# Layer 1's expert input weights read four rows to a partition, norm columns in that order, in a two-layer trunk kernel

## The chip, the cores and the metric

One core of a Trainium2 chip. The time is device microseconds of one execution. Before the change it was 2333.3 us (median of three runs, 2330.22 to 2333.62).

## The reference

A trunk of two layers on 1024 tokens of 1024 features, all in float32. Layer 0 has a pooling mixer, layer 1 chunked gated linear attention, and each is followed by a mixture of 64 experts. Cut to what matters here:

```python
for i in range(DEPTH):
    mod = (silu(c) @ w_mod[i] + b_mod[i])[:, None, :]
    shift1, scale1, gate1, shift2, scale2, gate2 = jnp.split(mod, 6, axis=-1)
    h = rmsnorm(x, norm_gain[i, 0]) * (1.0 + scale1) + shift1
    x = x + gate1 * (pool_mixer(h, ...) if i % 2 == 0 else gla_mixer(h, ...))
    h = rmsnorm(x, norm_gain[i, 1]) * (1.0 + scale2) + shift2
    x = x + gate2 * hier_moe(h, w_group, b_group, w_expert, b_expert, w_in, w_out)
return rmsnorm(x, final_norm_g)

def hier_moe(h, ...):          # top-1 of 8 groups, top-2 of its 8 experts for each token
    ...
    xs = t[token_of]           # tokens sorted by expert
    gu = lax.ragged_dot(xs, w_in, group_sizes)        # w_in: 1024 x 768 an expert
    gate, up = jnp.split(gu, 2, axis=-1)
    ys = lax.ragged_dot(silu(gate) * up, w_out, group_sizes)   # w_out: 384 x 1024
    ys = ys * weights.reshape(-1)[order][:, None]
    return jnp.zeros_like(t).at[token_of].add(ys)
```

The product with w_in sums over the 1024 features, so the features may be taken in any order if tokens and weights have the same one.

## The kernel before

The kernel works layer by layer: mixer, router, experts. A norm makes tokens without scale and shift, which go to a table h_d in DRAM; the per-feature scale (1 + scale2) times gain and the shift are kept as columns, feature on the partition, eight columns of 128 (`modA[:, l, 1, :]` and `sec(l, 3)`), and are applied behind the transposes in front of an expert. The sums are kept in DRAM, in x_d, to which each expert adds.

An expert is handled in a pass over at most 64 of its tokens; experts with more (the kernel looks at the counts that the router left) have a second pass. In layer 1, 64 experts make 68 passes. In one pass:

- POOL's `gather` (line 470) reads the tokens' rows from h_d into one of eight buffers XG: partitions 0 to 63 hold the features 0 to 511, partitions 64 to 127 the features 512 to 1023.
- `expert_in` has four transposes of 128x128 on PE (line 480), each of 128 consecutive columns of XG, and applies scale and shift to the results, on ACT for odd (line 488) and on DVE for even ones (line 490).
- `expert_first` has 32 matmuls with w_in (line 506), gate and up on the two halves of the partitions. ACT makes the SiLU (line 513), DVE the product with up (line 514).
- `expert_turn` transposes the hidden values on PE (line 522; its three read every third column, a step of 12 B) and ACT copies them (line 523). `expert_last` has 12 matmuls with w_out (line 531).
- DVE scales the result by the router's weight (line 536), and POOL adds the rows to x_d with a scatter (line 537).

On PE the order is written out: the next expert's transposes stand between its matmuls of `expert_first` and those of `expert_turn`, while ACT and DVE make the hidden values. On the other engines a scheduler orders the instructions at build time. On POOL, one scatter waits until the scatter before it has landed, since both add to x_d, and the gather for eight experts later stands between two scatters, since it writes the buffer that the scatter has read out. Gathers for second passes, where there is one, are made under a branch, `na` experts ahead (4).

The weights come on SP's queue, three loads of 1.573 MB an expert into a ring of 14 slots of 128 x 3072 floats: w_in in two halves (line 466) and w_out (line 467). A partition of a w_in slot gets four rows of w_in that lie 128 rows apart, in four runs of 3,072 B; a partition of w_out gets three consecutive rows, one run of 12,288 B. `queued` holds each load until the load three before it has landed, so that gathers and scatters find room on the DMA engines, which both share with the loads. Loads for layer 1's first experts are made while the mixer still runs (`fill1`).

In layer 1's mixer a loop over t handles eight tiles of 128 tokens, with the router one or two tiles behind; PE is in written order here too. Tokens of the tiles go through DRAM, and POOL fetches them with gathers (qk_d on line 1105, v_d on line 1109, r_d on line 1113, x_d on line 1114).

Of the kernel before, what the change touches and what calls it, by code (L numbers as in the profile page):

```python
# [36 lines left out]
def trunk_kernel(ctx, tc, x_in, c_in, norm_gain, w_mod, b_mod, pool_w, pool_b, pool_scale,  # L37
# [15 lines left out]
    v_d = dram.tile([SEQ, 1024], F32, name="v_d")  # L53
    r_d = dram.tile([SEQ, 1024], F32, name="r_d")
    z_d = dram.tile([SEQ, 16], F32, name="z_d")

    def part(slot, kb, n):
        a = int(kb * 256)
# [2 lines left out]
    def ps():  # L61
        return psum.tile([128, 512], F32, name="ps")
# [101 lines left out]
    def mod_scale(l, s):  # L164
        V.scalar_tensor_tensor(modA[:, l, s, :], mod[:, l, 24 * s + 8:24 * s + 16], 1.0,
                               C1[:, 96 + (2 * l + s) * 8:96 + (2 * l + s) * 8 + 8], op0=OP.add, op1=OP.mult)

    def sec(l, s):
        return mod[:, l, 8 * s:8 * s + 8]

    def row(col, half, diag):
        d = diag.rearrange("p (a b) -> p a b", a=4)
# [273 lines left out]
    hv = h_d.rearrange("t (g d) -> (t g) d", g=2)  # L446
    yv = [y.rearrange("t (g d) -> (t g) d", g=2) for y in x_d]

    def expert_load(win, wout, sl):
        behind.clear()  # L450
        for j in range(3):
            third_load(win, wout, j, sl)

    behind = []

    def queued(ins):

        if len(behind) >= DEEP:
            tc.add_manual_dep(ins.ins, behind[-DEEP].name, DATA_SYNC, reason="loads leave room for gathers")
        behind.append(ins.ins)  # L460
        return ins

    def third_load(win, wout, j, sl):
        if j < 2:
            src = win.rearrange("(k p) f -> p k f", p=128)
            return [queued(SP.dma_start(A[sl[j]].rearrange("p (k f) -> p k f", k=4), src[:, 4 * j:4 * j + 4]))]
        return [queued(SP.dma_start(A[sl[2]], wout.rearrange("(p c) d -> p (c d)", c=3)))]
# [8 lines left out]
    def expert_in(l, i, g, first=None):  # L476
        xT = part(15, 2 * i, 512).rearrange("p (c g t) -> p c g t", c=4, g=2)
        pp = [ps(), ps()]
        for cc in range(4):
            T.transpose(pp[cc % 2][:, cc // 2 * 128:cc // 2 * 128 + 128], XG[g][:, cc * 128:(cc + 1) * 128], ident)  # L480
        with tc.issue_after(first()) if first else ExitStack():
            for cc in range(4):
                pv = pp[cc % 2][:, cc // 2 * 128:cc // 2 * 128 + 128].rearrange("p (g t) -> p g t", g=2)
                for g in range(2):
                    kc = 4 * g + cc
                    sc, sh = modA[:, l, 1, kc:kc + 1], sec(l, 3)[:, kc:kc + 1]
                    if cc % 2:
                        S.activation(xT[:, cc, g, :], pv[:, g, :], AF.Identity, bias=sh, scale=sc)  # L488
                    else:
                        ins = V.tensor_scalar(xT[:, cc, g, :], pv[:, g, :], sc, sh, op0=OP.mult, op1=OP.add).ins  # L490
        return ins
# [146 lines left out]
    def rest(l, lo, hi, flag, src, sl, bufs):  # L638

        bi, bg = bufs  # L640
        base, en = ov[:, 0:1], ov[:, 1:2]
        pb, R, w = ov[:, 2:10], ov[:, 10:34], ov[:, 34:35]
        Rv = R.rearrange("p (t w) -> p t w", w=3)
        Sl = A[sl[0]][:, 0:512]
        nmax = nc.values_load(flag, min_val=0, max_val=SEQ, skip_runtime_bounds_check_because=COUNT_REASON)
        with tc.If(nmax > 128):
            V.memset(en, float(lo))
            with tc.For_i(lo, hi, 1) as e:
                n = nc.values_load(cnt_i[0:1, bass.ds(e, 1)], min_val=0, max_val=SEQ,
                                   skip_runtime_bounds_check_because=COUNT_REASON)  # L650
                with tc.If(n > 128):
                    V.memset(base, 128.0)
                    with tc.For_i(128, n, 64):
                        p = ps()
                        m = 0
                        for k in range(2):
                            V.tensor_scalar(pb, pos(k), base, None, op0=OP.subtract)
                            slots_of(Sl, pb, 0)
                            V.tensor_scalar(pb, eid(k), en, None, op0=OP.is_equal)
                            for c, a in enumerate((tokno, place, wk(k))):  # L660
                                V.tensor_tensor(Rv[:, :, c], pb, a, op=OP.mult)
                            for t in range(NT):
                                for g in range(2):
                                    T.matmul(p[64 * g:64 * g + 64, 0:3], Sl[:, t * 64:(t + 1) * 64], Rv[:, t, :],
                                             start=m == 0, stop=m == 15)
                                m += 1
                        V.tensor_scalar(ovi, p[:, 0:2], 2.0, gcol, op0=OP.mult, op1=OP.add)
                        V.tensor_copy(w, p[:, 2:3])
                        gather(ovi[:, 0:1], bg)
                        expert_in(l, bi, bg)  # L670
                        expert_load(*src(e), sl)
                        expert_out(l, bi, sl, (w, ovi[:, 1:2]), bg)
                        V.tensor_scalar(base, base, 64.0, None, op0=OP.add)
                V.tensor_scalar(en, en, 1.0, None, op0=OP.add)
# [128 lines left out]
    def load0(e, j, sl):  # L803
        r = e // 8
        if r not in regs:
            regs[r] = nc.values_load(cnt_i[0:1, NE + 16 + r:NE + 17 + r], engines=(ET.SP,), min_val=0, max_val=56,
                                     skip_runtime_bounds_check_because="eight times the number of a group")
        d = bass.ds(regs[r] + e % 8, 1)
        third_load(moe_w_in[0, d].rearrange("o k f -> (o k) f"), moe_w_out[0, d].rearrange("o k f -> (o k) f"), j, sl)

    for s in range(3):
        load0(0, s, RING0[0:3])
# [452 lines left out]
    pulled = [gl_load2(0), gl_load2(1)]  # L1265

    def load1(e, j, sl):
        return third_load(moe_w_in[1, e], moe_w_out[1, e], j, sl)

    def fill1(lo, hi):  # L1270
        for s in range(lo, hi):
# [20 lines left out]
    with tc.manual_schedule(engines={ET.PE}):  # L1292
        for t in range(NT + 2):
            for i in ((0, 1) if t == 0 else (t,) if 1 < t < NT else ()):
                gl_scores(i)
                if t == 0:
                    gl_mix(i)
            if t == 3:
                columns = [late_mod(14, LATE[4])]
            if t == 4:  # L1300
                columns = [late_mod(15, LATE[5])]
            if 0 < t < NT - 1:
                gl_z(t + 1)
            if t == 1:
                columns = [late_mod(10, LATE[0])]
            if t == 2:
                columns = [late_mod(12, LATE[2]), late_mod(13, LATE[3])]
            if 0 < t <= NT:
                gl_out(t - 1, 0)
            while columns:  # L1310
                columns.pop(0)()
            if t == 2:
                mod_scale(1, 1)
            if t > 1:
                route_turn(t - 2, 1, xnb, hTb)
            if t > NT:
                route_logits(t - 2, hTb, wrv, L, brow)
            if 0 < t < NT - 1:
                gl_gate(t + 1)
            if 1 < t < NT:  # L1320
                route_logits(t - 2, hTb, wrv, L, brow)
            if t == NT - 1:
                consts = route_consts(area1)
                r_a = route(1, 0, NT - 2, area1, consts, **held)
                r_b = route(1, NT - 2, NT, area2, consts, **held)
                next(r_a)
            if 1 < t < NT:
                gl_mix(t)
            if t == 1:
                columns = [late_mod(11, LATE[1])]  # L1330
            if t == NT - 1:
                gate2_rows(1, [part(8, 0, 512), part(8, 2, 512)])
            if 0 < t <= NT:
                gl_out(t - 1, 1)
                while columns:
                    columns.pop(0)()
                if t in (3, 4):
                    fill1(3 * t - 9, 3 * t - 6)
                SP.dma_start(x_d[1][(t - 1) * 128:t * 128, :], X[t - 1])
                xn_tile(t - 1, xnb, xnb, 3)  # L1340
            if t == NT:
                route_logits(t - 2, hTb, wrv, L, brow)
                next(r_a)
            if t < NT:
                gl_turn(t)
            if t + 2 < NT:
                gl_load(t + 2)
                gl_load_v(t + 2)
                gl_load2(t + 2)
# [14 lines left out]
                      reason="what is needed sooner goes first")  # L1364
    G.memset(part(15, 7, 1024), 0.0)
    with tc.manual_schedule(engines={ET.PE}):
        moe(1, RING1, MAIN1, (4, 5, 10, 11), load1, AHEAD1, 4)
    rest(1, 0, NE, cnt_i[0:1, NE + 8:NE + 9],
         lambda e: tuple(w[1, bass.ds(e, 1)].rearrange("o k f -> (o k) f") for w in (moe_w_in, moe_w_out)),
         RING1[0:3], (0, 4))  # L1370
# [43 lines left out]
```

## Time and profile before

| | us |
|---|---|
| median of three runs | 2333.3 |
| profiled execution | 2333.5 |
| its span | 2331.8 |
| PE busy | 1983.0 (85%) |
| weight loads of PE busy | 949.8 (41%) |
| DVE busy | 725.9 (31%) |
| ACT busy | 627.2 (27%) |
| POOL busy | 496.3 (21%) |

The span runs from the first to the last instruction; the time of the execution has 1.7 us more. Layer 1's experts take from about 1508 to 2302 us. Behind them the last scatter lands, the result is read back, normed and written. The mean granted clock of TensorE was 0.968 of full speed. Busy shares are means over stages with different limits, so the rows below are of single stages: a window row has the stretch, its length, the busy us of PE, weight loads, DVE, ACT and POOL with their counts, the granted clock, the busy share of the 16 DMA engines and their GB/s. In a timeline row, the figure in brackets is the time that the engine was idle before, with what ended it.

### The profile page before, as it was taken

Reading aid. Unit: us, or ns where it says so; the run is one execution under the profiler, and the core shown is the slowest. Engines: PE = TensorE matmul, PEld = TensorE weight load, DVE = VectorE, ACT = ScalarE, POOL = GpSimd, SP = SyncE. Lnnn points to the kernel's source line nnn. Section 1 sums busy time; section 2 is a strip of 40 time slices with the busy share of each in tenths; the row PEclk is TensorE's granted clock in tenths of the full one; section 3 lists DMA queues with packets and bytes.
Section 4 is the critical chain, followed back from the end, with each engine's and each line's share of the span. In section 5 each row is a group of like instructions: output and inputs, shape, how many; then the busy total and the mean of one; then the engine's idle time right before and its main releaser. Section 6 shows DMA issues by size and latency. Waiting matters only on the chain. (4 is left out here: it accounts for less than half of the span.)

```text
span 2331.8 us, 31439 instructions
## 1 busy us (share of the span) xinstructions
PE 1983.0 (85%) x11243; PEld 949.8 (41%) x11244; DVE 725.9 (31%) x1797; ACT 627.2 (27%) x1433; POOL 496.3 (21%) x422
## 2 busy tenths in 40 slices
PE   7867888899999999999888999888877777778784
PEld 5544333344444444444335665433323333333331
DVE  4463545312121221212137667422212111112122
ACT  4131323222222221313126665222111111112113
POOL 0303222222222222222115110222222212222210
PEclk9988999899999999999998999899999999999997
DMA  9999989998988899999945942699999999999995
GB/s 333 332 329 360 391 289 343 373 354 312 348 311 305 328 358 335 378 331 363 352 139 179 334 157 100 248 394 388 400 381 396 375 379 390 379 387 381 393 381 206
DMA packets 241991, 770.04 MB, mean 330 GB/s; under 512 B 31591, under 2 KB 63757, under 8 KB 224318
## 3 DMA queue, kind: packets, MB, share of 16 engines
q1 hardware_dynamic: 196498, 684.66, 76.1%
q0 software_dynamic: 43856, 77.67, 12.1%
q10 hardware_dynamic: 1372, 4.28, 0.5%
q8 instruction: 154, 2.52, 0.4%
q14 instruction: 111, 0.91, 0.1%
HBM read 735.44 MB, written 69.80 MB: 345 GB/s over the span
## 5 line engine op out<-in xcount | busy, mean ns | idle before, releaser
L506 PE MATMUL ps<-slot,slot 128*64 128x384 f32 x4416 | 755.4, 492 | 94.7 <-DMA slot<-in_moe_w_in_dram 76.5
L506 PEld LDWEIGHTS ps<-slot,slot 128*64 128x64 f32 x4416 | 337.0, 138 | 515.9 <-issue 248.3
L531 PE MATMUL ps<-slot,slot 128*64 128x512 f32 x1656 | 402.8, 623 | 49.3 <-ACT slot L523 42.8
L513 ACT ACTIVATE slot<-ps 64x384 f32<-64x384 f32 x138 | 66.9, 485 | 1261.6 <-PE ps L506 1235.6
L924 PE MATMUL ps<-slot,slot 128*128 128x512 f16 x1152 | 276.4, 386 | 7.2 <-DVEq L1061 5.7
L490 DVE TENSOR_SCALAR slot<-ps,kept 128x64 f32<-128x64 f32 x552 | 151.2, 334 | 339.7 <-PE ps L480 335.6
L514 DVE TENSOR_TENSOR slot<-slot,ps 64x384 f32<-64x384 f32 x138 | 75.9, 550 | 525.5 <-ACT slot L513 512.5
L537 POOL DMA_INDIRECT x_d<-kept x96 | 159.3, 1659 | 348.7 <-DVEq L632 172.4
L531 PEld LDWEIGHTS ps<-slot,slot 128*64 128x64 f32 x1656 | 110.7, 141 | 247.5 <-issue 184.4
L470 POOL DMA_INDIRECT kept<-h_d,kept x96 | 102.0, 1062 | 503.1 <-DMA x_d<-kept 328.3
L488 ACT ACTIVATE slot<-ps,kept 128x64 f32<-128x64 f32 x552 | 178.4, 403 | 70.0 <-PE ps L480 61.4
L536 DVE SCALAR_TENSOR_TENSOR kept<-ps,kept 128x512 f32<-128x512 f32 x96 | 72.0, 750 | 325.3 <-PE ps L531 322.5
L924 PEld LDWEIGHTS <-slot 128*128 128x128 f16 x1152 | 107.6, 99 | 153.4 <-issue 46.1
L522 PE MATMUL ps<-kept,slot 64*128 64x64 f32 x414 | 75.9, 290 | 91.9 <-DVE slot L514 90.6
L522 PEld LDWEIGHTS ps<-kept,slot 64*128 64x128 f32 x414 | 57.8, 202 | 135.8 <-DVE slot L514 101.0
L537 POOL DMA_INDIRECT x_d<-slot,kept x42 | 66.7, 1587 | 163.0 <-DVE slot L536 105.1
L470 POOL DMA_INDIRECT slot<-h_d,kept x42 | 43.8, 1042 | 243.8 <-DMA x_d<-slot,kept 158.4
L1236 PE MATMUL ps<-slot,slot 128*128 128x512 f16 x384 | 85.7, 379 | 1.2 <-DVE slot L1228 1.0
L536 DVE SCALAR_TENSOR_TENSOR slot<-ps,kept 128x512 f32<-128x512 f32 x42 | 31.5, 751 | 122.2 <-PE ps L531 116.3
L480 PE MATMUL ps<-kept 128*128 128x128 f32 x384 | 63.4, 288 | 1.6 <-DMA kept<-h_d,kept 1.3
L480 PEld LDWEIGHTS ps<-kept 128*128 128x128 f32 x384 | 40.6, 141 | 59.1 <-issue 56.7
L1236 PEld LDWEIGHTS <-slot 128*128 128x128 f16 x384 | 37.1, 98 | 46.6 <-issue 2.1
(329 smaller groups left out, 1693.2 us busy)
## 6 DMA issues: line engine op xcount, KB each, us to landing
slot<-in_moe_w_in_dram SPq DMA_DIRECT2D x256, 1536.0 KB
slot<-in_moe_w_out_dram SPq DMA_DIRECT2D x128, 1536.0 KB
slot<-in_w_mod_dram SPq DMA_DIRECT2D x30, 1536.0 KB
slot<-in_gla_w_in_dram SPq DMA_DIRECT2D x8, 1536.0 KB
h_d<-slot POOLq DMA_DIRECT2D x16, 512.0 KB
slot<-in_x_dram SPq DMA_DIRECT2D x8, 512.0 KB
slot<-x_d POOLq DMA_DIRECT2D x8, 512.0 KB
slot<-in_gla_w_out_dram SPq DMA_DIRECT2D x8, 512.0 KB
```

Source lines behind the costliest of these rows:

```text
L470: return G.indirect_dma_start(out=XG[i], out_offset=None, in_=hv, in_offset=bass.IndirectOffsetOnAxis(ap=idx, axis=0), bounds_check=2 * SE ...
L480: T.transpose(pp[cc % 2][:, cc // 2 * 128:cc // 2 * 128 + 128], XG[g][:, cc * 128:(cc + 1) * 128], ident)
L488: S.activation(xT[:, cc, g, :], pv[:, g, :], AF.Identity, bias=sh, scale=sc)
L490: ins = V.tensor_scalar(xT[:, cc, g, :], pv[:, g, :], sc, sh, op0=OP.mult, op1=OP.add).ins
L506: T.matmul(p1[s, 0:384], xT[:, cc, g, :], W[:, u], start=n == 0, stop=n == 7)
L514: return V.tensor_tensor(hh, hh, p1[up, 0:384], op=OP.mult).ins
L522: T.transpose(p3[:, cc * 64:(cc + 1) * 64], hh[:, :, cc], ident[s, s])
L531: T.matmul(p2[g * 64:g * 64 + 64, :], hT[:, cc * 64:(cc + 1) * 64], o[:, cc, g * 512:(g + 1) * 512], start=cc == 0, stop=cc == 2)
L536: V.scalar_tensor_tensor(XG[y], p2, w, G2, op0=OP.mult, op1=OP.mult)
L537: ins = G.indirect_dma_start(out=yv[l], out_offset=bass.IndirectOffsetOnAxis(ap=sidx, axis=0), in_=XG[y], in_offset=None, bounds_check=2 * ...
L924: T.matmul(p, hP[:, m, kc, :], W[:, n, :], start=kc + i == 0, stop=kc == KC - 1 and i == 2)
L1236: T.matmul(p, oT[:, m, kc, :], woh[kc][:, n, half * 512:(half + 1) * 512], start=kc + i == 0, stop=kc == KC - 1 and i == 2)
```

## The change

In layer 1 alone, partition p of a w_in slot now gets four consecutive rows of w_in (4p to 4p + 3 of a half), one run of 12,288 B in place of four of 3,072 B. The tokens' features must come in the same order: each transpose in front of an expert reads every fourth column of XG (a step of 16 B), and the columns of scale and shift must be in that order too. `mod_turn`, called in the mixer's loop at t = 3, makes them: it transposes both sets of eight columns on PE, copies them on DVE, writes them to a small DRAM table m_d and reads them back in the new order into the columns of layer 0, which are no longer used. `expert_in` reads these columns in both layers. The gathers for second passes are made three experts ahead in layer 1, not four.

```diff
--- before.py
+++ after.py
@@ -53,6 +53,7 @@
     v_d = dram.tile([SEQ, 1024], F32, name="v_d")
     r_d = dram.tile([SEQ, 1024], F32, name="r_d")
     z_d = dram.tile([SEQ, 16], F32, name="z_d")
+    m_d = dram.tile([2, 8, 128], F32, name="m_d")
 
     def part(slot, kb, n):
         a = int(kb * 256)
@@ -167,6 +168,17 @@
 
     def sec(l, s):
         return mod[:, l, 8 * s:8 * s + 8]
+
+    def mod_turn(l, scr):
+
+
+        p = ps()
+        T.transpose(p[0:8, 0:128], modA[:, l, 1, :], ident)
+        T.transpose(p[0:8, 128:256], sec(l, 3), ident)
+        V.tensor_copy(scr[0:8, :], p[0:8, 0:256])
+        G.dma_start(m_d.rearrange("v k p -> k v p"), scr[0:8, :].rearrange("k (v p) -> k v p", v=2))
+        for v, a in enumerate((modA[:, 0, 1, :], sec(0, 3))):
+            G.dma_start(a.rearrange("p (g c) -> p g c", g=2), m_d[v].rearrange("(g b) (a c) -> (b a) g c", g=2, c=4))
 
     def row(col, half, diag):
         d = diag.rearrange("p (a b) -> p a b", a=4)
@@ -446,10 +458,10 @@
     hv = h_d.rearrange("t (g d) -> (t g) d", g=2)
     yv = [y.rearrange("t (g d) -> (t g) d", g=2) for y in x_d]
 
-    def expert_load(win, wout, sl):
+    def expert_load(l, win, wout, sl):
         behind.clear()
         for j in range(3):
-            third_load(win, wout, j, sl)
+            third_load(l, win, wout, j, sl)
 
     behind = []
 
@@ -460,7 +472,10 @@
         behind.append(ins.ins)
         return ins
 
-    def third_load(win, wout, j, sl):
+    def third_load(l, win, wout, j, sl):
+
+        if j < 2 and l:
+            return [queued(SP.dma_start(A[sl[j]], win.rearrange("(g p k) f -> p g (k f)", g=2, k=4)[:, j]))]
         if j < 2:
             src = win.rearrange("(k p) f -> p k f", p=128)
             return [queued(SP.dma_start(A[sl[j]].rearrange("p (k f) -> p k f", k=4), src[:, 4 * j:4 * j + 4]))]
@@ -477,13 +492,14 @@
         xT = part(15, 2 * i, 512).rearrange("p (c g t) -> p c g t", c=4, g=2)
         pp = [ps(), ps()]
         for cc in range(4):
-            T.transpose(pp[cc % 2][:, cc // 2 * 128:cc // 2 * 128 + 128], XG[g][:, cc * 128:(cc + 1) * 128], ident)
+            rows = XG[g].rearrange("p (r c) -> p c r", c=4)[:, cc] if l else XG[g][:, cc * 128:(cc + 1) * 128]
+            T.transpose(pp[cc % 2][:, cc // 2 * 128:cc // 2 * 128 + 128], rows, ident)
         with tc.issue_after(first()) if first else ExitStack():
             for cc in range(4):
                 pv = pp[cc % 2][:, cc // 2 * 128:cc // 2 * 128 + 128].rearrange("p (g t) -> p g t", g=2)
                 for g in range(2):
                     kc = 4 * g + cc
-                    sc, sh = modA[:, l, 1, kc:kc + 1], sec(l, 3)[:, kc:kc + 1]
+                    sc, sh = modA[:, 0, 1, kc:kc + 1], sec(0, 3)[:, kc:kc + 1]
                     if cc % 2:
                         S.activation(xT[:, cc, g, :], pv[:, g, :], AF.Identity, bias=sh, scale=sc)
                     else:
@@ -668,7 +684,7 @@
                         V.tensor_copy(w, p[:, 2:3])
                         gather(ovi[:, 0:1], bg)
                         expert_in(l, bi, bg)
-                        expert_load(*src(e), sl)
+                        expert_load(l, *src(e), sl)
                         expert_out(l, bi, sl, (w, ovi[:, 1:2]), bg)
                         V.tensor_scalar(base, base, 64.0, None, op0=OP.add)
                 V.tensor_scalar(en, en, 1.0, None, op0=OP.add)
@@ -806,7 +822,7 @@
             regs[r] = nc.values_load(cnt_i[0:1, NE + 16 + r:NE + 17 + r], engines=(ET.SP,), min_val=0, max_val=56,
                                      skip_runtime_bounds_check_because="eight times the number of a group")
         d = bass.ds(regs[r] + e % 8, 1)
-        third_load(moe_w_in[0, d].rearrange("o k f -> (o k) f"), moe_w_out[0, d].rearrange("o k f -> (o k) f"), j, sl)
+        third_load(0, moe_w_in[0, d].rearrange("o k f -> (o k) f"), moe_w_out[0, d].rearrange("o k f -> (o k) f"), j, sl)
 
     for s in range(3):
         load0(0, s, RING0[0:3])
@@ -1265,7 +1281,7 @@
     pulled = [gl_load2(0), gl_load2(1)]
 
     def load1(e, j, sl):
-        return third_load(moe_w_in[1, e], moe_w_out[1, e], j, sl)
+        return third_load(1, moe_w_in[1, e], moe_w_out[1, e], j, sl)
 
     def fill1(lo, hi):
         for s in range(lo, hi):
@@ -1311,6 +1327,8 @@
                 columns.pop(0)()
             if t == 2:
                 mod_scale(1, 1)
+            if t == 3:
+                mod_turn(1, part(4, 11, 256))
             if t > 1:
                 route_turn(t - 2, 1, xnb, hTb)
             if t > NT:
@@ -1364,7 +1382,7 @@
                       reason="what is needed sooner goes first")
     G.memset(part(15, 7, 1024), 0.0)
     with tc.manual_schedule(engines={ET.PE}):
-        moe(1, RING1, MAIN1, (4, 5, 10, 11), load1, AHEAD1, 4)
+        moe(1, RING1, MAIN1, (4, 5, 10, 11), load1, AHEAD1, 3)
     rest(1, 0, NE, cnt_i[0:1, NE + 8:NE + 9],
          lambda e: tuple(w[1, bass.ds(e, 1)].rearrange("o k f -> (o k) f") for w in (moe_w_in, moe_w_out)),
          RING1[0:3], (0, 4))
```

On SP, among the first loads of layer 1's experts in the mixer, the order stays and the form of the w_in loads changes. x_d is the table of sums, and slots are numbered by the program. Before:

```order
L466 DMA slot_69<-in_moe_w_in_dram 128x4x768
L467 DMA slot_73<-in_moe_w_out_dram 128x3072
L466 DMA slot_79<-in_moe_w_in_dram 128x4x768
L1339 DMA x_d<-slot_72 128x1024
L466 DMA slot_78<-in_moe_w_in_dram 128x4x768
```

And now:

```order
L478 DMA slot_69<-in_moe_w_in_dram 128x3072
L482 DMA slot_73<-in_moe_w_out_dram 128x3072
L478 DMA slot_79<-in_moe_w_in_dram 128x3072
L1357 DMA x_d<-slot_72 128x1024
L478 DMA slot_78<-in_moe_w_in_dram 128x3072
```

No load has moved; a partition's four runs have become one.

On POOL, in the mixer at t = 3, before (h_d, qk_d, v_d, r_d and x_d are tables in DRAM, "kept" holds row numbers here):

```order
L215 DMA h_d<-slot_71 128x1024
L1114 DMA slot_72<-x_d,kept 128x1024
L1105 DMA slot_74<-qk_d,kept 128x1024
L1109 DMA slot_72<-v_d,kept 128x1024
L1113 DMA slot_80<-r_d,kept 128x1024
L1114 DMA slot_80<-x_d,kept 128x1024
```

And now:

```order
L227 DMA h_d<-slot_71 128x1024
L1130 DMA slot_72<-x_d,kept 128x1024
L179 DMA m_d<-slot_70 8x2x128
L1121 DMA slot_74<-qk_d,kept 128x1024
L181 DMA kept<-m_d 128x2x4 x2
L1125 DMA slot_72<-v_d,kept 128x1024
L1129 DMA slot_80<-r_d,kept 128x1024
L1130 DMA slot_80<-x_d,kept 128x1024
```

The store of the columns stands ahead of the gather from qk_d, and the two that read them back ahead of the gather from v_d; the rest is as before.

## Rows read from the trace of the kernel before

**Rows 1.** windows: us; busy us (count) by engine; clock; DMA share; GB/s

```profile
1300.00:1360.00 60.00, 60.00 (x420) 35.99 (x420) 37.90 (x98) 39.02 (x70) 9.54 (x11) 1.00 0.78 292
...
1660.00:1760.00 100.00, 75.68 (x400) 30.82 (x396) 18.89 (x48) 16.47 (x48) 22.73 (x17) 0.98 1.02 388
```

**Rows 2.** DMA queues, 1530 to 2270 us: packets, MB, share

```profile
q1 hardware_dynamic: 68513, 269.30, 92.6%
```

**Rows 3.** SP's queue waits, 1530 to 2270: us, times, longest

```profile
SPq L466 <- DMA slot<-in_moe_w_in_dram: 444.8, 113, 6.0
...
SPq L467 <- DMA slot<-in_moe_w_out_dram: 206.8, 53, 5.6
```

**Rows 4.** timeline, SP at 1508 and PE at 2191: start, us, instruction, wait

```profile
1508.01 1.28 SPq L467 DMA_DIRECT2D slot<-in_moe_w_out_dram  x1
...
2191.03 0.54 PE L506 MATMUL ps<-slot,slot 128*64 128x384 f32 x2 [1.39 <-DMA slot<-in_moe_w_in_dram]
```

**Rows 5.** timeline of DVE line 536, four of the 68 passes

```profile
1689.75 0.75 DVE L536 SCALAR_TENSOR_TENSOR kept<-ps,kept 128x512 f32<-128x512 f32 x1 [2.90 <-PE ps L531]
...
2093.87 0.75 DVE L536 SCALAR_TENSOR_TENSOR kept<-ps,kept 128x512 f32<-128x512 f32 x1 [2.83 <-PE ps L531]
...
2280.72 0.75 DVE L536 SCALAR_TENSOR_TENSOR slot<-ps,kept 128x512 f32<-128x512 f32 x1 [2.79 <-PE ps L531]
...
2301.00 0.75 DVE L536 SCALAR_TENSOR_TENSOR slot<-ps,kept 128x512 f32<-128x512 f32 x1 [3.86 <-PE ps L531]
```

**Rows 6.** DMA packets, 1659 to 1662 and 1672.5 to 1675.5

```profile
DMA packets 404, 1.21 MB, mean 403 GB/s; under 512 B 13, under 2 KB 13, under 8 KB 403
...
DMA packets 401, 1.20 MB, mean 400 GB/s; under 512 B 10, under 2 KB 10, under 8 KB 401
```

**Rows 7.** DMA packets, 1820.5 to 1822.5 and 2160.5 to 2162.5

```profile
DMA packets 92, 0.84 MB, mean 420 GB/s; under 512 B 3, under 2 KB 3, under 8 KB 30
...
DMA packets 92, 0.83 MB, mean 415 GB/s; under 512 B 5, under 2 KB 5, under 8 KB 31
```

**Rows 8.** lines by form, 1560 to 2260: busy us, mean ns; idle before

```profile
L480 PEld LDWEIGHTS ps<-kept,slot 128*128 128x128 f32 x120 | 12.6, 140 | 17.9 <-issue 17.9
...
L522 PEld LDWEIGHTS ps<-kept,slot 64*128 64x128 f32 x174 | 24.3, 202 | 54.3 <-DVE slot L514 53.4 <-issue 0.9
```

**Rows 9.** timeline of PE, one pass near the end

```profile
2276.86 0.56 PE L522 MATMUL ps<-kept,slot 64*128 64x64 f32 x3 [0.70 <-DVE slot L514]
```

**Rows 10.** timeline of POOL in the mixer

```profile
1339.86 0.94 POOL L1105 DMA_INDIRECT slot<-qk_d,kept  x1 [0.33 <-PE ps L1135]
...
1348.23 1.05 POOL L1109 DMA_INDIRECT slot<-v_d,kept  x1 [7.42 <-DVE slot L1151]
```

**Rows 11.** timeline of POOL among the experts

```profile
1598.92 1.60 POOL L537 DMA_INDIRECT x_d<-kept  x1 [0.30 <-issue]
...
1671.55 1.04 POOL L470 DMA_INDIRECT slot<-h_d,kept  x1 [9.82 <-DMA x_d<-slot,kept]
...
1729.02 1.04 POOL L470 DMA_INDIRECT kept<-h_d,kept  x1 [7.87 <-PE ps L531]
...
2283.43 1.55 POOL L537 DMA_INDIRECT x_d<-slot,kept  x1 [9.33 <-DMA x_d<-slot,kept]
...
2302.03 1.55 POOL L537 DMA_INDIRECT x_d<-slot,kept  x1 [8.54 <-DVE slot L536]
```

**Rows 12.** DMA packets during three waits of POOL, and from 2284

```profile
DMA packets 486, 1.95 MB, mean 390 GB/s; under 512 B 105, under 2 KB 105, under 8 KB 395
...
DMA packets 579, 1.40 MB, mean 311 GB/s; under 512 B 103, under 2 KB 103, under 8 KB 576
...
DMA packets 294, 1.66 MB, mean 369 GB/s; under 512 B 33, under 2 KB 33, under 8 KB 193
...
DMA packets 147, 0.16 MB, mean 39 GB/s; under 512 B 81, under 2 KB 81, under 8 KB 145
```

**Rows 13.** chain that ended last, the last scatter

```profile
2302.03 4.16 DMA x_d<-slot,kept
```

## Prediction

> **What bounds the kernel now.** I read the stretches first [rows 1]. In layer 1's mixture of experts the DMA engines are busy 1.02 of the time at 388 GB/s, while PE is busy 75.68 of 100 us: transfers, not arithmetic, hold this stage. The queue view says whose they are [rows 2]: the loads' queue q1 has 92.6% of the 16 engines. Then SP, which issues the loads [rows 3]: of 740 us it waits 444.8 + 206.8 = 651.6 us for the landing of an earlier load, and next to nothing for a free slot. So a chain of loads runs, each let go by the load three before it. It restarts at 1508.01 (expert 4's w_out, load 14 counted from 0), and PE waits for it for the last time at 2191.03, for expert 56's second w_in, load 169 [rows 4]. That is 156 loads in 683 us, 4.38 us each; 104 of them are w_in (experts 5 to 56, two each). DVE's scaling of a pass's result shows what PE pays [rows 5]: from 1689.75 to 2093.87 there are 31 passes of 13.04 us, from 2280.72 to 2301.00 two of 10.14. The latter is the pass without waits, so 31 × 2.9 = 90 us of waiting lie in that stretch alone: room to take a faster load chain in. The eleven passes behind 2191.03 (experts 56 to 63, three of them with a second pass: 110 us / 10.14 = 10.8) are PE's own and move as a block. From 1508 to 2191 a microsecond off the chain is therefore a microsecond off the end, if nothing else takes over.
>
> **The change, part by part.** *The w_in loads.* 1.573 MB move in 128 runs of 12,288 B rather than 512 of 3,072 B; w_out has long been moved so. In two stretches with w_in alone (403 of 404 and 401 of 401 packets under 8 KB) the engines move 403 and 400 GB/s [rows 6]; in two stretches mostly of w_out, 420 and 415 [rows 7]. 1.573 / 401.5 GB/s = 3.92 us, 1.573 / 417.5 = 3.77: 0.15 us a load. From below: SP's mean wait for a landing is 3.94 us for w_in (444.8/113) and 3.90 for w_out (206.8/53) [rows 3], no more than 0.04 apart; but three loads are under way at once, and the intervals smear the kinds. So 0 is the low end. From above: in the w_out stretches 30 of 92 packets still are small; without them the rate would be a little higher, and I allow 0.25. I take 0.15, from rates of the very transfers in question: 104 × 0.15 = 15.6 us gained, between 0 and 26.
>
> The Trainium skill, "DMA: Bandwidth & Descriptors", section "Why small descriptors are slow (HBM only)", charges some 3 cycles a packet beside one cycle per 32 B: 99 cycles for 96 at 3,072 B, 387 for 384 at 12,288 B. That is 2.3%, an estimate of 0.09 us a load and 9.4 us in all; the rates above are 4% apart, so the measurement gives more, and the sum goes by the measurement.
>
> *The transposes in front of an expert* (L480) now read every fourth float. This trace has no step of 16 B, but has one of 12 B: L522's weight loads take 202 ns, L480's contiguous ones 140 [rows 8]. Four a pass at 62 ns more are 0.25 us; as low end 0, as high end 1.5 times that, 0.37, since the step is longer. They lie ahead of DVE L514, for which PE then waits 0.70 us before the next transposes [rows 9]; a longer L480 is mostly absorbed there. I take 0.1 us for each of the eleven passes behind the last wait for weights, 1.1 us (0 to 4); in the passes before them the 2.9 us of waiting for weights hides it.
>
> The Trainium skill, "SBUF — State Buffer", Door 1, in its note on cachelines, says that lines have 16 B and that each access which crosses to a new one pays. By that the new step hits a new line with every element, where the step of 12 B now and then hits one twice, which speaks for the upper half of my interval; fully paid it would make the term 4 us instead of 1.1.
>
> *The columns in the new order.* Two transposes of 8 columns, one DVE copy of 8 × 256, a store and two reloads in pieces of 16 B. In the mixer PE is busy 60.00 of 60 us [rows 1], so the two transposes are on the path: at two weight loads of L480's 140 ns some 0.3 us, and 0.1 for whoever waits on the copy: 0.4 (0 to 2). The three DMAs go on POOL's queue ahead of the v_d gather; that gather waits 7.42 us for DVE today, behind the qk_d gather [rows 10], and three issues of the 1.0 us class fit into it. If they don't, up to 2 us are lost there, and x_d's gather behind them is late by as much. The columns are needed only when the experts start, some 160 us on.
>
> *Overflow gathers three experts ahead.* Costed at nothing: three passes are 30 us, and the longest wait for a transfer in the rows is 9.82 us [rows 11]. One branch and, at most, one gather less stand ahead of the first scatter.
>
> *The sum.* The profiled execution took 2333.5 us (span 2331.8 and 1.7 around it), against a median of 2333.3, so nothing is to be shifted: 2333.5 − 15.6 + 1.1 + 0.4 = 2319.4, forecast 2319.
>
> **What may be late next: POOL's chain.** After an expert's scatter POOL waits a time W until it has landed, makes a gather (1.04 + 0.31 us) and then the next scatter (1.60). From the scatter of 1598.92 to that of 2302.03 there are 59 such cycles, 52 with gathers [rows 11]. W grows when the engines carry long packets: 7.87 us where 3 of 579 packets are long, 9.82 where 91 of 486 are (57% of the bytes), 9.33 where 101 of 294 are (75%) [rows 12]. Once loads have ended (39 GB/s from 2284) a scatter lands 4.16 us after its start [rows 12, 13]. If the loads end 16 us earlier, by 2268, POOL has 2268 − 1598.92 − 52 × 1.35 = 599 us for loaded cycles of 1.60 + W, and the rest go at 4.16. With W = 9.33, the row nearest to an all-long queue, 54.8 cycles are done by 2268 and 4.2 remain: last scatter 2285, about PE's new end (2302 − 16 = 2286). So PE just still decides, and everything above 9.33 shows.
>
> The Trainium skill, "DMA: Bandwidth & Descriptors", section "Queues, rings and completion order", says that an engine goes round its queues packet by packet. By that rule a scatter's small packet always waits for one load packet, four times as long after the change; the growth of W in the rows agrees with it, and rival D is its consequence.
>
> **Rivals.** *B, POOL decides but late by less than the gain.* Extrapolating 7.87 and 9.33 to 100% long bytes gives 7.87 + 1.46/0.75 = 9.8. Then 599/11.4 = 52.5 cycles, 6.5 × 4.16 = 27, last scatter 2295: 7 us gained, 2326. For it: the extrapolation. Against it: the step from 57% to 75% shows no growth.
>
> *C, the long runs aren't faster.* SP's landing intervals are the same for both kinds; the w_out rates might come from where in the stage those stretches lie. Then only 1 to 2 us change: 2333.5 + 1.5 − 3 = 2332. Against it: two stretches of each kind agree within 5 GB/s.
>
> *D, slower, by POOL's chain.* Extrapolating 7.87 and 9.82 gives 7.87 + 1.95/0.57 = 11.3; take W = 10.4. A cycle with gather is then 13.35 us, longer than PE's pass, and its lag outgrows the eight gather buffers: PE waits for rows. The gather for the last expert comes behind 51 cycles, 1598.92 + 681 = 2280, and eight scatters at 4.16 follow: 2313, 11 us after today's, 2345. It decides from about W = 10.1. For it: one row at 9.82 already with a third of the loads long. Against it: the row with the most long bytes has 9.33.
>
> **How the numbers follow.** The forecast has 0.50, with a range of its own from 2308 (26 us gained) to 2328 (6 gained); B 0.20, C 0.12, D 0.18. A measurement of this kernel tells 0.2%, 4.7 us, from no change. Faster: 0.48 of the forecast, 0.16 of B, 0.02 of C, 0.66. Same: 0.02, 0.04 and 0.09, 0.15. Slower: D and 0.01 of C, 0.19. From 2308 to 2338 the range leaves out most of D and the best of the forecast.
>
> **What would show it.** Right: the w_in stretches move some 415 GB/s; 31 passes of about 12.7 us where 13.04 stood; PE's last wait for weights about 16 us earlier; eleven passes of 10.1 to 10.3 behind it; the last DVE L536 followed at once by its scatter. L480's weight loads between 200 and 240 ns. Wrong: if PE's idle time in L480 is ended by gathers, or if the last scatter comes long after its L536, with W over 9.8, POOL has taken over; if load intervals keep 4.38 us, C holds; if the mixer ends more than 2 us later, the columns were not hidden.

## The result, and the profile after

The changed kernel takes 2351.3 us (median of 4 runs, 2346.5 to 2352.5) against 2331.8 us for the kernel before (4 runs): ratio 1.0083, 95% interval 1.0055 to 1.0111. It is slower; 2319 with a range of 2308 to 2338 was forecast. Its profiled execution has a span of 2344.8 us, 13.0 more than that of before.

The first group of rows is the window view of the changed kernel, with the columns of [rows 1]; L485, L553 and L552 below are the lines 470, 537 and 536 of before, L496 and L522 the lines 480 and 506.

```profile
1660.00:1760.00 100.00, 83.69 (x457) 36.06 (x455) 21.15 (x54) 17.88 (x54) 21.13 (x16) 1.00 1.00 404
2000.00:2100.00 100.00, 58.62 (x304) 24.63 (x302) 14.15 (x36) 11.91 (x36) 21.11 (x16) 0.86 1.01 402
```

Where [rows 1] had 388 GB/s and 75.68 us of PE there are 404 GB/s and 83.69 us: the loads are faster. But from 2000 to 2100 PE works 58.62 us of 100, while the DMA engines stay full (the last figures of a row are granted clock, DMA share and GB/s). DVE's scaling of the passes' results, beside [rows 5], shows the same in passes:

```profile
1513.75 0.75 DVE L552 SCALAR_TENSOR_TENSOR kept<-ps,kept 128x512 f32<-128x512 f32 x1 [5.37 <-PE ps L547]
...
1688.88 0.75 DVE L552 SCALAR_TENSOR_TENSOR kept<-ps,kept 128x512 f32<-128x512 f32 x1 [2.93 <-PE ps L547]
...
2059.16 0.75 DVE L552 SCALAR_TENSOR_TENSOR slot<-ps,kept 128x512 f32<-128x512 f32 x1 [2.93 <-PE ps L547]
2099.04 0.75 DVE L552 SCALAR_TENSOR_TENSOR kept<-ps,kept 128x512 f32<-128x512 f32 x1 [5.04 <-PE ps L547]
...
2181.27 0.75 DVE L552 SCALAR_TENSOR_TENSOR slot<-ps,kept 128x512 f32<-128x512 f32 x1 [2.92 <-PE ps L547]
2211.11 0.75 DVE L552 SCALAR_TENSOR_TENSOR kept<-ps,kept 128x512 f32<-128x512 f32 x1 [5.60 <-PE ps L547]
...
2313.67 0.75 DVE L552 SCALAR_TENSOR_TENSOR slot<-ps,kept 128x512 f32<-128x512 f32 x1 [3.87 <-PE ps L547]
```

From 1688.88 to 2059.16 there are 30 passes of 12.34 us, where before had 31 of 13.04. Then two single gaps: 39.88 us at the first pass of expert 48, and 29.84 at that of expert 56, both experts with a second pass. Taking a pass of 12.34 for each, that is 27.5 + 17.5 = 45.0 us lost at these two places. Without them the last row would be at 2268.6, 32 us ahead of the 2301.00 of before; with them it is 12.7 behind. This estimate is somewhat high, since the loads go on while PE stands and the passes behind a stop then take 10.3 us: pool_in_order below, which has no such stop, has its last row at 2274.37. The wait view of PE names what it stood for, and its timeline the two places:

```profile
PE ps L496 <- DMA slot<-h_d,kept: 42.6, 2, 25.5
```

```profile
2056.31 2.79 PE L547 MATMUL ps<-slot,slot 128*64 128x512 f32 x12 [0.48 <-ACT slot L539]
...
2091.97 1.10 PE L496 MATMUL ps<-kept,slot 128*128 128x128 f32 x4 [25.50 <-DMA slot<-h_d,kept]
...
2094.73 4.26 PE L547 MATMUL ps<-slot,slot 128*64 128x512 f32 x12 [1.11 <-ACT slot L539]
...
2203.48 1.10 PE L496 MATMUL ps<-kept,slot 128*128 128x128 f32 x4 [17.10 <-DMA slot<-h_d,kept]
```

It waited for gathered rows, not for weights. The waits are 42.6 of the 45.0 us. While PE stood, its granted clock fell to 0.50 (1.2 GHz), and it was still there right behind the first stop: the twelve matmuls with w_out at 2094.73 took 4.26 us, against 2.79 at 2056.31. POOL's timeline up to the first stop, the counterpart of [rows 11]:

```profile
2054.12 1.60 POOL L553 DMA_INDIRECT x_d<-kept  x1 [0.30 <-issue]
2065.87 1.04 POOL L485 DMA_INDIRECT kept<-h_d,kept  x1 [10.15 <-DMA x_d<-kept]
2067.21 1.60 POOL L553 DMA_INDIRECT x_d<-kept  x1 [0.30 <-issue]
2078.10 1.04 POOL L485 DMA_INDIRECT kept<-h_d,kept  x1 [9.29 <-DMA x_d<-kept]
2079.45 1.60 POOL L553 DMA_INDIRECT x_d<-slot,kept  x1 [0.30 <-issue]
2082.29 1.04 POOL L485 DMA_INDIRECT slot<-h_d,kept  x1 [1.24 <-issue]
```

From scatter to scatter POOL takes 13.09 and 12.24 us here, and 12.96 as a mean from pass 17 to 47 (passes are counted from 0), more than a pass of 12.34. POOL doesn't wait for DVE: each scatter goes out 0.30 us behind a gather that has waited for the landing of the scatter before. Over passes 8 to 55, W (from a scatter's end to POOL's next gather or scatter) has a mean of 9.97 us, where before had 8.46; the few scatters behind which a gather went out without waiting (W under 3 us) are left out, 4 of 48 here and 2 before. At 2059.9 DVE has finished pass 47, but POOL's scatter of 2054.12 is that of pass 42. The scatter of pass 47 goes out at 2118.1, 58.2 us after its data are ready; before, the longest such lag was 18.8 us, and at pass 47 it was 0.3. Most of the lag is old: by pass 17 it is 39.8 us, since the first passes, with weights loaded ahead, take 10.29 us each. The kernel before builds up its 18.8 us by pass 16 in the same way and loses them by pass 27, because its passes of 13.04 us are longer than its scatter cycle (11.34 us from pass 17 to 27). With long runs the passes became shorter and the cycle longer, so the lag stayed and grew. The gather of 2082.29 brings the rows of expert 48's second pass. PE asks for them from about 2066.

### The profile page after: what moved, and what is told of

It is laid out like the page before. It is cut to its first block, busy times and chain, and to the rows that moved or that the text cites. A ratio compares the mean times of both kernels' runs of the same rounds, so it can differ in the third digit from the quotient of the medians.

```text
span 2344.8 us, 31455 instructions
## 1 busy us (share of the span) xinstructions
PE 1990.2 (85%) x11245; PEld 959.8 (41%) x11246; DVE 725.8 (31%) x1798; ACT 622.9 (27%) x1433; POOL 496.7 (21%) x425
## 5 line engine op out<-in xcount | busy, mean ns | idle before, releaser
L522 PE MATMUL ps<-slot,slot 128*64 128x384 f32 x4416 | 750.5, 490 | 68.0 <-DMA slot<-in_moe_w_in_dram 51.6
L522 PEld LDWEIGHTS ps<-slot,slot 128*64 128x64 f32 x4416 | 334.5, 137 | 483.7 <-issue 256.8
L547 PE MATMUL ps<-slot,slot 128*64 128x512 f32 x1656 | 410.7, 633 | 52.4 <-ACT slot L539 48.3
L553 POOL DMA_INDIRECT x_d<-kept x96 | 158.4, 1650 | 325.7 <-DVEq L648 168.6
L485 POOL DMA_INDIRECT kept<-h_d,kept x96 | 101.6, 1058 | 555.7 <-DMA x_d<-kept 321.7
L552 DVE SCALAR_TENSOR_TENSOR kept<-ps,kept 128x512 f32<-128x512 f32 x96 | 72.0, 750 | 337.3 <-PE ps L547 334.4
L940 PEld LDWEIGHTS <-slot 128*128 128x128 f16 x1152 | 107.9, 100 | 154.5 <-issue 47.4
L485 POOL DMA_INDIRECT slot<-h_d,kept x42 | 43.8, 1042 | 276.3 <-DMA x_d<-slot,kept 174.7
L553 POOL DMA_INDIRECT x_d<-slot,kept x42 | 67.1, 1598 | 112.9 <-DVE slot L552 58.5
L496 PE MATMUL ps<-kept,slot 128*128 128x128 f32 x168 | 31.8, 314 | 45.0 <-DMA slot<-h_d,kept 45.0
L552 DVE SCALAR_TENSOR_TENSOR slot<-ps,kept 128x512 f32<-128x512 f32 x42 | 31.5, 751 | 123.1 <-PE ps L547 117.0
L496 PEld LDWEIGHTS ps<-kept 128*128 128x128 f32 x384 | 44.7, 163 | 58.2 <-issue 57.6
L496 PE MATMUL ps<-kept 128*128 128x128 f32 x384 | 65.9, 294 | 1.3 <-DMA kept<-h_d,kept 1.3
```

The lines of the kernel that those rows point to most:

```text
L485: return G.indirect_dma_start(out=XG[i], out_offset=None, in_=hv, in_offset=bass.IndirectOffsetOnAxis(ap=idx, axis=0), bounds_check=2 * SE ...
L522: T.matmul(p1[s, 0:384], xT[:, cc, g, :], W[:, u], start=n == 0, stop=n == 7)
L547: T.matmul(p2[g * 64:g * 64 + 64, :], hT[:, cc * 64:(cc + 1) * 64], o[:, cc, g * 512:(g + 1) * 512], start=cc == 0, stop=cc == 2)
L552: V.scalar_tensor_tensor(XG[y], p2, w, G2, op0=OP.mult, op1=OP.mult)
L553: ins = G.indirect_dma_start(out=yv[l], out_offset=bass.IndirectOffsetOnAxis(ap=sidx, axis=0), in_=XG[y], in_offset=None, bounds_check=2 * ...
L940: T.matmul(p, hP[:, m, kc, :], W[:, n, :], start=kc + i == 0, stop=kc == KC - 1 and i == 2)
```

## The experiments

Each ratio is of a kernel's runs to those of the kernel before on the same chip. "Lag" is the time from DVE's result to its scatter; W and lag are those of the one profiled execution of each kernel. W is left empty where POOL's gather doesn't wait for the landing.

| kernel | median us (before) | ratio, 95% interval | mean W, us | longest lag, us |
|---|---|---|---|---|
| changed kernel | 2351.3 (2331.8) | 1.0083, 1.0055 to 1.0111 | 9.97 | 58.2 |
| lead8 | 2354.0 (2337.5) | 1.0061, 1.0041 to 1.0081 | 9.97 | 61.1 |
| before_lead4 | 2337.2 (2337.5) | 1.0000, 0.9983 to 1.0017 | 8.32 | 16.2 |
| short_runs | 2335.6 (2337.5) | 1.0000, 0.9979 to 1.0020 | 8.18 | 14.6 |
| long_runs_only | 2348.6 (2337.5) | 1.0049, 1.0034 to 1.0065 | 9.91 | 59.9 |
| pool_in_order | 2307.8 (2330.7) | 0.9898, 0.9861 to 0.9935 | | 8.9 |
| before_pool_in_order | 2326.6 (2330.7) | 0.9970, 0.9947 to 0.9993 | | 1.4 |
| half_runs | 2318.8 (2330.7) | 0.9938, 0.9917 to 0.9958 | 8.82 | 19.5 |
| no_second_pass | 2313.0 (2330.7) | 0.9921, 0.9873 to 0.9969 | 10.14 | 67.2 |
| lead5 | 2345.1 (2337.2) | 1.0036, 1.0016 to 1.0057 | 10.30 | 55.4 |
| pool_and_sp | 2315.3 (2337.2) | 0.9911, 0.9892 to 0.9931 | | 9.7 |
| pool_and_half_runs | 2317.7 (2337.2) | 0.9919, 0.9892 to 0.9946 | | 2.0 |

**Which edit costs.** Four kernels take the change apart. lead8 undoes the shorter lead of the second passes' gathers:

```diff
-        moe(1, RING1, MAIN1, (4, 5, 10, 11), load1, AHEAD1, 3)
+        moe(1, RING1, MAIN1, (4, 5, 10, 11), load1, AHEAD1, 4)
```

> The changed kernel with the gathers for second passes four experts ahead as before (in POOL's order, eight passes before they are needed and not four). Theory: long load packets make W about 9.9 us and POOL lags up to 58 us, and the two stalls of PE of 25.5 and 17.1 us come only from the shorter lead; without them about 2318 us (2308 to 2328), with W still near 9.9 and no wait of PE for a gather over 3 us. Rival 1, POOL's chain alone sets the end: 2340 or more, with the last scatters late. Rival 2, the cost lies in the transposes and columns: 2350.

before_lead4 makes the reverse edit (4 to 3) in the kernel before.

> The kernel before with the gathers for second passes three experts ahead and nothing else changed. Theory: with short load packets POOL's lag is at most 19 us and near 0 at the experts concerned, so the shorter lead costs nothing: 2332 (2327 to 2337). Rival, the lead alone costs: 2345 to 2360, with PE waiting for a gather.

short_runs takes the two added lines out of `third_load` of the changed kernel:

```diff
-        if j < 2 and l:
-            return [queued(SP.dma_start(A[sl[j]], win.rearrange("(g p k) f -> p g (k f)", g=2, k=4)[:, j]))]
```

> The changed kernel with w_in loaded in runs of 3,072 B as before, all else changed (the products then pair features in different orders, so the values are not the reference's). Theory: W back to about 8.1 us, no stall of PE for a gather, and only the columns cost: 2335 (2331 to 2340), 31 DMA-bound passes of about 13 us again. Rival, transposes and columns carry the loss: 2350.

long_runs_only puts these two lines into the kernel before, and nothing else.

> The kernel before with w_in loaded in runs of 12,288 B and nothing else changed (the products pair features in different orders, so the values are not the reference's). Theory: W about 9.9 us, lag over 50 us, but with the lead of eight passes no stall: 2314 (2304 to 2324), some 4 us less than the changed kernel with the longer lead. Rival, long runs cost by POOL's chain whatever the lead: 2335 or more.

Columns, transposes and lead together cost nothing that can be measured (short_runs, 1.0000, within 0.2%), nor does the lead alone (before_lead4). The long runs alone bring a loss of 0.5%, with W at 9.91 and a lag of 59.9 us; the 0.6% of lead8 can't be told from it. That part of the theory held. But two expectations failed: lead8 took 2354, not 2318, and long_runs_only 2349, not 2314. The longer lead doesn't help. PE stood still at the same two places, although the gather for expert 48 now went out four passes earlier. POOL's and PE's timelines of lead8:

```profile
2041.12 1.60 POOL L553 DMA_INDIRECT x_d<-kept  x1 [0.30 <-DVE slot L530]
2043.77 1.03 POOL L485 DMA_INDIRECT slot<-h_d,kept  x1 [1.05 <-issue]
...
2090.96 1.60 POOL L553 DMA_INDIRECT x_d<-slot,kept  x1 [0.30 <-issue]
```

```profile
2095.18 0.68 PE L496 MATMUL ps<-kept,slot 128*128 128x128 f32 x2 [19.07 <-DMA slot<-h_d,kept]
```

The gather of 2043.77 stands behind the scatter of pass 40, and PE starts its transposes at 2095.18 all the same, just behind the scatter of pass 44. The program offers a reason: with four buffers, the buffer of expert 48 is also that of expert 52, and with four experts ahead the branch that would fill it for 52 stands in the program before 48's second pass. PE must wait until POOL has passed that branch, behind the scatter of pass 44, whether it fills the buffer or not. This is argued from the program and not shown: the row names only a gather that had gone out 51 us before. By it, both kernels let PE be about four passes ahead of POOL there. long_runs_only, with the lead of lead8, has two such waits as well:

```profile
PE ps L482 <- DMA slot<-h_d,kept: 33.4, 2, 21.2
```

**Is it the lag behind POOL's chain?** The next theory: W grows with the length of the packets between which a scatter's small ones must pass; POOL's chain of scatter, landing, gather, scatter becomes longer than a pass; the lag reaches four passes; and the second passes are where it first shows. pool_in_order takes the gather's wait out of the chain. POOL keeps the written order in layer 1's experts, and a gather is made six experts ahead, into a buffer whose scatter landed before the last one went out:

```diff
-    with tc.manual_schedule(engines={ET.PE}):
-        moe(1, RING1, MAIN1, (4, 5, 10, 11), load1, AHEAD1, 3)
+    with tc.manual_schedule(engines={ET.PE, ET.Pool}):
+        for e in (4, 5):
+            gather(ig[:, 0, e:e + 1], MAIN1[e])
+        moe(1, RING1, MAIN1, (4, 5, 10, 11), load1, 6, 3)
```

> The changed kernel with POOL's instructions of layer 1's experts in written order, gathers six experts ahead: a gather then goes out between two scatters without waiting for the first to land. Theory: W for long packets is a queueing time, and the chain scatter, landing, gather, scatter of 12.9 us a pass is what makes POOL lag; without the gather's wait the cycle is 10.6 to 11.5 us, less than a DMA-bound pass of 12.3, so no lag over 25 us, no stall at the second passes: 2308 (2300 to 2322), 28 us under before. Rival, the DMA engines have no room for both whatever the order: lag and stalls stay, 2340 to 2355.

POOL's timeline of it:

```profile
1908.43 1.60 POOL L553 DMA_INDIRECT x_d<-kept  x1 [9.19 <-DVE kept L552]
1910.78 1.05 POOL L485 DMA_INDIRECT kept<-h_d,kept  x1 [0.75 <-issue]
1921.49 1.60 POOL L553 DMA_INDIRECT x_d<-slot,kept  x1 [9.67 <-DMA x_d<-kept]
1923.88 1.04 POOL L485 DMA_INDIRECT kept<-h_d,kept  x1 [0.79 <-issue]
1934.45 1.62 POOL L553 DMA_INDIRECT x_d<-slot,kept  x1 [9.53 <-DVE slot L552]
```

The gather now goes out 0.75 us behind the scatter, during its landing, and the next scatter waits for DVE's result about as often as for the landing. The lag stays under 9 us, no wait for a gather is left, and the kernel is 1.0% faster than before with the very loads that made it slower. The same order in the kernel before:

> The kernel before with the same written order on POOL. Theory: with short packets POOL doesn't hold the kernel, so nothing is won: 2335 (2328 to 2340). Rival, POOL's order matters by itself: 2325 or less, or 2345 or more.

It wins 0.3%, just outside the range expected of it, and much less than the 1.0% with long runs. The two kernels in written order differ in the change alone: over passes 17 to 47 a pass takes 12.90 us with short runs and 12.42 with long ones, 14.4 us in all. Up to pass 17 PE doesn't wait for loads in either, but the chain of loads has run since load 14, so this is the gain of the 86 w_in loads of experts 5 to 47: 0.17 us each.

half_runs changes the length of the packets: two runs of 6,144 B, the transposes reading every second column, the columns in that order:

```diff
...
-            return [queued(SP.dma_start(A[sl[j]], win.rearrange("(g p k) f -> p g (k f)", g=2, k=4)[:, j]))]
+            return [queued(SP.dma_start(A[sl[j]].rearrange("p (h f) -> p h f", h=2), win.rearrange("(g h p k) f -> p g h (k f)", g=2, h=2, k=2)[:, j]))]
...
-            rows = XG[g].rearrange("p (r c) -> p c r", c=4)[:, cc] if l else XG[g][:, cc * 128:(cc + 1) * 128]
+            rows = XG[g].rearrange("p (h r c) -> p h c r", h=2, c=2)[:, cc // 2, cc % 2] if l else XG[g][:, cc * 128:(cc + 1) * 128]
```

> The changed kernel with two runs of 6,144 B to a partition in place of one of 12,288, and the tokens' features and columns in that order. Theory: W between 8.4 and 9.9, about 8.9 us, cycle 11.9 us, lag 30 to 45 us, stalls at second passes under 8 us each: 2322 (2312 to 2335). Rival, it is the new layout and not the length of packets: as the changed kernel, 2350.

W is 8.82 us, between 8.46 and 9.97. The lag stays at 19.5 us, less than was expected, and no stall is left. So W follows the length of the packets (with the long ones it is 9.91 to 10.30 in the five kernels of the table); the new layout as such does no harm.

no_second_pass leaves the stalls no place:

```diff
-                with tc.If(count(e, pool_only) > 64):
+                with tc.If(count(e, pool_only) > (SEQ - 1 if l else 64)):
...
-                              count(e, engines) > 64, tos[1], more(e), aside or (lambda *marks: None))
+                              count(e, engines) > (SEQ - 1 if l else 64), tos[1], more(e), aside or (lambda *marks: None))
```

> The changed kernel without second passes in layer 1: tokens beyond 64 of an expert are left out, 4 passes of 68. Theory: the stalls are bound to second passes, so all of them go although POOL's lag stays near 58 us or grows: PE's work ends about 2255, POOL's last scatter 20 to 30 us later, 2312 (2300 to 2322), 40 us of passes and nothing else being left out. Rival, PE is held by the lag at the other gathers too: 2330 or more, with waits for gathers of single passes.

The kernel leaves out 4 of the 68 passes. The time is as expected, but its rival has a part in it (the profiled execution took 2323.0 us, 10 more than the median). The wait view of PE has

```profile
PE ps L496 <- DMA slot<-h_d,kept: 10.5, 6, 3.3
PE ps L496 <- DMA kept<-h_d,kept: 8.8, 8, 2.2
```

14 short waits at ordinary gathers, 19 us in all, so a lag that grows on (67.2 us here) reaches the first passes' buffers too. And POOL ends behind PE: DVE's last result is there at 2269.51, the last scatter goes out at

```profile
2290.54 1.57 POOL L553 DMA_INDIRECT x_d<-slot,kept  x1 [2.92 <-DMA x_d<-slot,kept]
```

lead5 gives the second passes a lead of five passes, at the cost of one buffer of the first ones:

```diff
-MAIN1, AHEAD1 = (0, 1, 2, 3, 6, 7, 8, 9), 4
+MAIN1, AHEAD1 = (0, 1, 2, 3, 6, 7, 8), 4
...
-        moe(1, RING1, MAIN1, (4, 5, 10, 11), load1, AHEAD1, 3)
+        moe(1, RING1, MAIN1, (4, 5, 10, 11, 9), load1, AHEAD1, 4)
```

> The changed kernel with five buffers for second passes and seven for first ones, so that a second pass's rows are waited for five passes behind POOL and not four. Theory: PE stalls there because it is four passes ahead of POOL; one pass more takes a POOL cycle, some 12.9 us, off the stall at expert 48 (25.5 us) and moves what follows forward by as much; the one at expert 56 stays near 17: 2338 (2330 to 2346). Rival, the stalls don't hang on the lead: 2350 with stalls as before.

The two long stalls shrink from 25.5 and 17.1 us to 6.9 each:

```profile
PE ps L496 <- DMA slot<-h_d,kept: 29.4, 8, 6.9
...
PE ps L496 <- DMA kept<-h_d,kept: 11.7, 6, 3.3
```

But the 41.1 us of all waits for gathers are nearly the 42.6 of the changed kernel, spread over 14 places; in PE's timeline from 1918 to 2066 they stand at first passes, which now have seven buffers. The ratio of 1.0036 is under the 1.0083 of the changed kernel, but the two intervals touch. So here the lead decided where PE waits, and POOL's chain how much.

Two combinations were tried for a faster version. pool_and_sp issues the columns' three DMAs from SP (`SP.dma_start` for `G.dma_start` in `mod_turn`); pool_and_half_runs joins POOL's order with the runs of half_runs.

> POOL in written order and, beside it, the columns' three DMAs issued by SP in place of POOL. Theory: the columns cost 3 to 4 us on POOL, since its qk_d gather waits behind the store for DVE's copy; on SP they cost nothing: 2304 (2298 to 2310). Rival, the columns cost elsewhere or nothing: 2308.

> POOL in written order with runs of 6,144 B. Theory: with POOL no longer in the way only the rate of the loads counts, and longer runs are the better ones: 2312 (2305 to 2320), some 4 us above POOL in order with runs of 12,288 B. Rival, shorter packets help the scatters so much that it is the best: 2300 or less.

pool_and_sp missed its range, pool_and_half_runs lies in it. Neither beats pool_in_order (0.9911 and 0.9919 against 0.9898, the intervals overlap), and the rival of half runs as the best is out. What the columns cost can't be settled so: the first scatter of the experts falls between 1509 and 1523 us in the kernels of this study, with no order by what they do to the columns. pool_in_order, with 0.9898, has the lowest ratio and beats both the kernel before and the changed one.

## Why the prediction was wrong, point by point

**The bound** was right: the chain of loads set the pace of passes 17 to 47, and a faster load was passed on to PE, as 83.69 for 75.68 us of [rows 1] show.

**The gain of the loads** was sized rightly: 0.15 us a load was forecast from two pairs of rate windows [rows 6, 7], and the pair in written order gives 0.17, over 86 loads. Its last scalings are 20.8 us apart (2295.16 with short runs, 2274.37 with long ones), its first ones 2.9. Between the changed kernel and the kernel before the loads gained more: pass 47 is scaled at 2059.16 against 2080.72. By then POOL had made 43 scatters in place of 47, so that the loads had less beside them; whether this is the reason was not tested. SP's landing intervals [rows 3], the reason for the low end and for rival C, showed nothing of the gain.

**The transposes and columns** were small, as forecast. L496's weight loads take 210 ns in the view by lines, where [rows 8] had 140 and 202:

```profile
L496 PEld LDWEIGHTS ps<-kept,slot 128*128 128x128 f32 x120 | 17.1, 210 | 60.6 <-issue 60.6
```

A pass without waits went from 10.27 to 10.29 us, so the 0.1 us a pass was too much. (The prediction's 10.14 is the mean of the last two passes, and the last has no next expert's transposes in it.) In the passes near the end the four transposes take 0.75 us for 0.66, and the wait behind them, for L514 [rows 9], fell from 0.70 to 0.61: it hid the price, as the prediction said. The Trainium skill, "SBUF — State Buffer", Door 1, has each access to a new line of 16 B pay. The row agrees that there is a price, 70 ns of a weight load. The columns are open: the first scaling came at 1513.75, where before had 1511.42, 2.3 us later and more than the 2 us that the prediction named as a sign, but the kernels of this study differ by more than that without a reason in the columns.

**POOL's chain** is the step that failed. It took W = 9.33, "the row nearest to an all-long queue", and let POOL lag freely until the loads have ended. W was 9.97, mis-sized by 0.64. By the prediction's own formula that alone would have given 599 / 11.57 = 51.8 cycles, 7.2 left at 4.16, a last scatter at 2298, still 4 us ahead of before. What the formula lacked is that PE may not run ahead of POOL by as much as the lag: rival D had this with the eight gather buffers and from W = 10.1, but at a second pass it is four passes, and 58 us are more than four passes. The step on the overflow gathers, "Costed at nothing: three passes are 30 us", compared the lead with the longest transfer, 9.82 us, and not with that transfer and POOL's lag together: PE waited 25.5 and 17.1 us there. A lead of four in place of three would not have saved it (lead8). So D was the rival that came true in its cause, PE waiting for rows because POOL lags, but with its place in the second passes and its point of decision lower. That its 2345 lies near the 2351 is luck: D had POOL's last scatters set the end, and here the last scatter goes out 0.3 us behind its scaling, after two stops of PE that D didn't have. For the gain of half_runs, W = 8.82 in the same formula was enough to be harmless, and so it was.

The Trainium skill, "DMA: Bandwidth & Descriptors", section "Queues, rings and completion order", was cited for the rule that an engine goes round its queues packet by packet. W of 8.46, 8.82 and 9.97 us for runs of 3,072, 6,144 and 12,288 B agrees with it in sign and order. W grew by 18% from the shortest to the longest, not fourfold as the prediction's one load packet did, and the page's packet is a group of descriptors, so its rule gives no size here. Which part of W is the gather's and which the scatter's own waiting was not measured.

## What to carry to other kernels

A transfer made more efficient by longer packets takes its gain from the latency of every small transfer on the same engines: work out the chain that hangs on such a latency (here scatter, landing, gather, scatter) in us a pass, and compare it with the new, shorter pass. A lag is built up where passes are short, and lost again only where they are longer than the chain. A lag that grows is harmless only up to the shortest lead of any buffer, that of a rare branch included; add lag and transfer before calling a lead long enough. Where a chain has become the bound, look first for a wait in it that a different order on the queue doesn't need: here one order turned 0.8% lost into 1.0% won.

## What the runs showed of the hardware that was not expected

Loads of 1.573 MB in runs of 12,288 B for 3,072 B raised the DMA engines' rate from 388 to 404 GB/s in the same window, and the time until a scatter of 128 rows of 2 KB lets POOL go on from 8.46 to 9.97 us. Runs of 6,144 B had about half of what the passes gained (12.68 us a pass over passes 17 to 47, between 13.03 and 12.34) for a quarter of that price (8.82 us). And a weight load that reads every fourth float took 210 ns, hardly more than one that reads every third (202, on 64 partitions), against 140 for contiguous ones.
